# A hybrid encoder step on one core: the scan's strip products in two bursts a group, the mask by 64-row products, two small pads

## The chip, the cores and the metric

The kernel runs on one core of one Trainium2 chip. The metric is the device time of one execution in microseconds. Shown are the median of three runs and one profiled execution with its trace. PE is TensorE (its matmuls; PEld its weight loads), DVE is VectorE, ACT is ScalarE, POOL is GpSimd, SP the engine whose queue issues most DMAs.

## The reference

One layer for a prompt of 1024 rows and a sample of 64 rows that share the weights. Three head groups read one projection of the normalised input; their gated outputs go through `w_out`, and a cross-attention to 256 memory rows follows. Cut to the two parts that the change touches:

```python
def hgrn2_scan(q, k, v, g, s0):                  # 4 heads of 128
    def step(s, inp):                            # one chunk of rows
        G = jnp.cumsum(gc, axis=1)
        o = jnp.einsum('bthk,bhkv->bthv', qc * jnp.exp(G), s)
        diff = G[:, :, None] - G[:, None, :]
        decay = jnp.exp(jnp.where(causal, diff, -jnp.inf))
        att = jnp.einsum('bthk,btshk,bshk->bhts', qc, decay, kc)
        o = o + jnp.einsum('bhts,bshv->bthv', att, vc)
        s_new = jnp.exp(GL)[..., None] * s + jnp.einsum('bshk,bshv->bhkv', kc * jnp.exp(GL[:, None] - G), vc)

def sb_block(q, q_pos, k, v, k_pos):             # 4 heads of 64
    z = jnp.einsum('bqhd,bkhd->bhqk', q, k) * (B_HEAD_DIM ** -0.5)
    mask = (k_pos[None, :] < q_pos[:, None])[None, None]
    log_1m = jnp.where(mask, jax.nn.log_sigmoid(-z), 0.0)
    after = lax.cumsum(log_1m, axis=3, reverse=True) - log_1m
    w = jnp.where(mask, jnp.exp(jax.nn.log_sigmoid(z) + after), 0.0)
    return jnp.einsum('bhqk,bkhd->bqhd', w, v)
```

Beside these stand the pooling group, the memory's keys and values (`mem_kv`, sixteen blocks of `w_xk` and `w_xv`), and `cross_attn`.

## The kernel before

**Stages.** The start transposes and splits the memory rows and the inputs and makes the memory's keys and values (up to about 100 us). Then come the input projections, with the scan of each head beside them (to about 455), the stick-breaking attention beside its own projections and `w_out` (to about 690), the cross-attention (to about 836) and `w_xo`. Every wide product is done as three fp32r products of split operands: `hhi,whi`, `hlo,whi` and `hhi,wlo`, 128 rows by 384, 320 or 256 columns.

**What sets the order.** `Sched` runs generators that record instructions: `main` and spawned tasks such as `hgrn0`. It keeps a virtual time for each engine, adds a cost for each recorded instruction, and gives the next turn to the first task whose dependences are done at PE's virtual time; a task gives up its turn at each `yield`. A projection yields after every six products. `pause(0.9)` yields until PE's virtual time is 0.9 us on. A list scheduler then places the recorded instructions on each engine in its own order, by priority and readiness. Loads of weight blocks go through SP's queue into two buffers `wraw`; ScalarE makes `whi` of them, VectorE `wlo`.

**A scan group.** A head has three groups: two of four chunks of 128 rows, and the sample's one chunk of 64. `prepA` and `prepB` make the factors `E` (one tile for each level), `k`, `qf`, `Kh` on ScalarE and VectorE. `pe1a` does the strip products of the two coarse levels into `pA`. `pe1b` does those of the four fine levels and of the diagonal, 16 and 4 for a chunk, each 32 columns of weights wide, into one PSUM tile `pB` for two chunks; VectorE multiplies and reduces `pB` to blocks of `AT`, ScalarE copies `pA` into `AT`. PE then transposes `Kh`, ScalarE copies the result to `Kt`. `pe2a` multiplies `V` by `Kt` and updates the states `S`; `pe2b` multiplies `V` by `AT` and `G` by `S` and norms the result (`o_sb`); `pe3` transposes `o_sb`. Before the change, `pe1b` pauses after each chunk, and the group pauses before `pe1b`.

**The mask.** `scores` multiplies, for two heads at once, rows 0 to 63 and rows 64 to 127 of the queries and keys (three products for each of two PSUM tiles `zs`). In the unit that holds the newest keys it adds a triangle of -1e30 by a product of an identity, `identb`, with `negmask`, over all 128 rows. There are 18 such units.

**Pools.** Tiles lie one behind another in pools. `const` holds `identb` and `negmask`; `C` and the transposed inputs `hT` follow it. `start` holds `mhi` and `mlo` (the memory rows, split), `xattn` the cross-attention's tiles.

Of the kernel before, what the change touches and what calls it, by code (L numbers as in the profile page):

```python
# [8 lines left out]
F32 = mybir.dt.float32  # L9
F32R = mybir.dt.float32r  # L10
BF16 = mybir.dt.bfloat16
AF = mybir.ActivationFunctionType
ALU = mybir.AluOpType
AX = mybir.AxisListType

P = 128
# [9 lines left out]
NEG = -1e30  # L26
# [78 lines left out]
def hybrid_step(  # L105
# [102 lines left out]
    with tc.high_priority(offset=10 * URGENT):  # L208
        ones = const([P, P], F32, "ones")
        DVE.memset(ones, 1.0)  # L210
        ident = const([P, P], F32, "ident")
        make_identity(nc, ident)
        mhalf = const([P, 4], F32, "mhalf")
        POOL.memset(mhalf, -0.5)

        identb = const([P, P], BF16, "identb")
        negmask = const([P, P], BF16, "negmask")
        DVE.memset(negmask, 0.0)
        POOL.affine_select(out=negmask, in_=negmask, pattern=[[-1, P]], compare_op=ALU.is_gt,
                           fill=NEG, base=0, channel_multiplier=1)  # L220
        cur["masks"] = (identb, negmask)
        blkmask = const([P, 4], F32, "blkmask")
        DVE.memset(blkmask, 0.0)
        for i in range(4):
            DVE.memset(blkmask[32 * i:32 * i + 32, i:i + 1], 1.0)
        invw = const([P, 2], F32, "invw")
        invcnt = const([P, 2, 16], F32, "invcnt")
        for ct in range(2):
            POOL.iota(invcnt[:, ct, :], pattern=[[1, 16]], base=1, channel_multiplier=0,
                      allow_small_or_imprecise_dtypes=True)  # L230
            for g in range(2):
                w = float(2 << (2 * ct + g))
                rs = slice(64 * g, 64 * g + 64)
                DVE.memset(invw[rs, ct:ct + 1], 1.0 / w)

    def late_constants(pool):
        wpl = pool([P, 2, P], F32, "wpl")
        DVE.memset(wpl, 0.0)
        DVE.tensor_copy(identb, ident)
        for ct in range(2):  # L240
            for g in range(2):
                rs = slice(64 * g, 64 * g + 64)
                DVE.tensor_scalar(out=invcnt[rs, ct, :], in0=invcnt[rs, ct, :], scalar1=float(2 << (2 * ct + g)),
                                  scalar2=None, op0=ALU.min)
        DVE.reciprocal(invcnt, invcnt)
        for g in range(4):
            rs = slice(64 * (g % 2), 64 * (g % 2) + 64)
            POOL.dma_start(wpl[rs, g // 2, rs], w_pool[0, g])
        onorm = const([P, 4], F32, "onorm")
        POOL.dma_start(onorm, hgrn_onorm_g)  # L250
        pscale = const([P, 2], F32, "pscale")
        POOL.dma_start(pscale, pool_scale)
        cur["hgrn"] = (blkmask, onorm)
        cur["pool"] = (invw, invcnt, wpl, pscale)
# [109 lines left out]
    def hgrn(h, st, hp, hgc):  # L364
# [103 lines left out]
        def pe1b(gi):  # L468

            t0, width, csz, v0 = groups[gi]  # L470
            nch, nq = width // csz, csz // 32
            x = ctxs[gi]
            E, k, qf, pA = x["E"], x["k"], x["qf"], x["pA"]
            AT = hp([P, 4, P], F32, "AT", 1)
            for c0 in range(0, nch, 2):
                cn = min(2, nch - c0)
                pB = ps_hg()[:, :384].rearrange("p (c l t) -> p c l t", l=6, t=32)
                for c in range(cn):
                    o = (c0 + c) * csz
                    for li, b in enumerate(FINE):  # L480
                        for i in range(nq):
                            sl = slice(o + 32 * i, o + 32 * i + 32)
                            mm(pB[32 * i:32 * i + 32, c, li, :], E[b][:, sl], E[b][:, sl], True, True)
                    for i in range(nq):
                        sl = slice(o + 32 * i, o + 32 * i + 32)
                        mm(pB[32 * i:32 * i + 32, c, 4:6, :], k[:, sl], qf[:, :, sl], True, True)
                    yield from pause(0.9)
                msk = hp([P, 2, 6, 32], F32, "msk")
                tt(msk[:csz, :cn].rearrange("p c l t -> p c (l t)"),
                   pB[:csz, :cn].rearrange("p c l t -> p c (l t)"),  # L490
                   fmask[:csz].rearrange("p l t -> p (l t)").unsqueeze(1).broadcast_to([csz, cn, 192]), ALU.mult)
                dg = hp([P, 2, 32], F32, "dg", 2)
                sch.op("DVE", 0.07 + cn * 192 / 960.0)
                DVE.tensor_reduce(out=dg[:csz, :cn], in_=msk[:csz, :cn].rearrange("p c l t -> p c t l"), axis=AX.X,
                                  op=ALU.add)
                tt(AT[:csz, c0:c0 + cn, :csz].rearrange("p c (i t) -> p c i t", t=32),
                   dg[:csz, :cn].unsqueeze(2).broadcast_to([csz, cn, nq, 32]),
                   blkmask[:csz, :nq].unsqueeze(1).unsqueeze(3).broadcast_to([csz, cn, nq, 32]), ALU.mult)
            if csz == P:
                act(AT[0:64, :nch, 64:128], pA[0:64, :nch, 64:128], AF.Copy)  # L500
            for s in range(0, csz, 64):
                act(AT[s:s + 32, :nch, s + 32:s + 64], pA[s:s + 32, :nch, s + 32:s + 64], AF.Copy)
            pk = ps_tp()
            for c in range(nch):
                tr(pk[:csz, c * P:(c + 1) * P], x["Kh"][:, c * csz:(c + 1) * csz], P)
            Kt = hp([P, 512], F32, "Kt")
            act(Kt[:csz, :nch * P], pk[:csz, :nch * P], AF.Copy)
            x["AT"], x["Kt"] = AT, Kt
# [62 lines left out]
        yield None  # L571
        pe1a(0)
        beside(prepA, 1)
        yield from pause(0.9)
        yield from pe1b(0)
        yield None
        pe2a(0, None)
# [7 lines left out]
        pe1a(1)  # L585
        beside(prepA, 2)
        factors_of(1)
        yield from pause(0.9)
        yield from pe1b(1)
        yield None  # L590
        pe2a(1, ctxs[0]["S"][-1])
# [7 lines left out]
        yield None  # L599
        pe1a(2)  # L600
        sch.done[("wide", h)] = 0.0
        yield from pause(0.9)
        yield from pe1b(2)
        yield None
        pe3(1)
# [2 lines left out]
        yield None  # L608
        pe2b(2)
        SP.dma_start(s_hgrn[0, 0, h], ctxs[2]["S"][-1])  # L610
        yield None
        pe3(2)

    def sb_all(ops, pool):
# [14 lines left out]
        def scores(u):  # L629
            (qh, ql), (kh, kl), vb, cv = ops[u["pair"]]  # L630
            i, n, nq = u["i"], u["n"], _rows(u["i"])
            u["s"], u["m"] = [], []
            zs = [ps_hg(), ps_hg()]
            qs = slice(i * P, i * P + nq)
            ks = slice(u["base"] + u["s0"], u["base"] + u["s0"] + n)
            for pi, (q, k) in enumerate(((qh, kh), (qh, kl), (ql, kh))):
                for e in range(2):
                    own = slice(64 * e, 64 * e + 64)
                    mm(zs[e][:nq, :n], q[own, qs], k[own, ks], pi == 0, pi == 2 and not u["first"])
            if u["first"]:  # L640
                for z in zs:
                    mm(z[:nq, n - nq:n], cur["masks"][0][:nq, :nq], cur["masks"][1][:nq, :nq], False, True)
            for e, z in enumerate(zs):
                s = pool([P, 512], F32, "sm", 7)
                m = pool([P, 512], F32, "sm", 7)
                act(m[:nq, :n], z[:nq, :n], AF.Sigmoid, scale=-0.125)
                act(s[:nq, :n], z[:nq, :n], AF.Sigmoid, scale=0.125)
                p = None if u["first"] else u["before"]["m"][e]
                sch.op("DVE", 0.07 + n / 480.0)
                DVE.tensor_tensor_scan(m[:nq, :n][:, ::-1], m[:nq, :n][:, ::-1], m[:nq, :n][:, ::-1],  # L650
                                       1.0 if p is None else p[:nq, 0:1], ALU.mult, ALU.min)
                if p is not None:
                    tt(s[:nq, n - 1:n], s[:nq, n - 1:n], p[:nq, 0:1], ALU.mult)
                tt(s[:nq, :n - 1], s[:nq, :n - 1], m[:nq, 1:n], ALU.mult)
                u["s"].append(s)
                u["m"].append(m)
# [76 lines left out]
    def main():  # L733
# [155 lines left out]
        g1 = pool([P, D], F32, "g1")  # L889
        g1row = pool([33, D], F32, "rows")[32:33]  # L890
        gT = pool([P, KT], F32, "gT")
        with tc.high_priority(offset=10 * URGENT):
            with nc.allow_non_contiguous_dma("one column per 128 of the norm's weights"):
                ACT.dma_start(gT, norm_mem.rearrange("o (k p) -> p (o k)", p=P))
            ACT.dma_start(g1row, norm_mix_pre)
# [434 lines left out]
        for h in range(4):  # L1330
# [14 lines left out]

            sch.fresh()
            kv = load_kv(h)
            wbs = [xw.pop(2 * h), xw.pop(2 * h + 1)]
            for c, (t0, n) in enumerate(CHUNKS):
                n1 = min(n, SEQ - t0)  # L1350
# [109 lines left out]
```

## Time and profile before

| | |
|---|---|
| median of three runs | 935.03 us (934.71 to 935.86) |
| the profiled execution | 935.02 us, its span 933.3 us |
| instructions | 18372 |
| PE busy | 914.2 us, 98% of the span |
| VectorE, ScalarE, POOL busy | 556.6, 479.5, 107.2 us |
| granted TensorE clock | 0.996 |
| DMA | 73.60 MB, 79 GB/s in the mean |

The span runs from the first to the last instruction; the execution's own time holds 1.7 us more. A row of the timeline gives the start, the duration, the engine and line, the operation, the tile written and those read, the rows and columns of a product with its shape, and the count of like instructions in a row. The ends of matmuls are modelled, and they overlap. In the trace a product of fp32 operands (`hg<-E`, `hg<-qf,k`, `hg<-V,Kt`) stands as two instructions, one of fp32r operands as one.

### The profile page before, as it was taken

The page shows a single profiled execution, that of the slowest core. Times are in us where ns is not written, and L with a number is a line of the kernel's source. Part 1 is how long each engine was busy: PE and PEld are TensorE (multiplying, and loading weights), DVE is VectorE, ACT ScalarE, POOL GpSimd, SP SyncE. Part 2 cuts the span into 40 slices and gives each one's busy share as a digit, 9 for nine tenths or more (in the row PEclk, how much of TensorE's full clock was granted, in tenths as well). Part 3 has the DMA queues.
Part 4 walks back from the last instruction along what each step waited for, and adds up shares of the span by engine and source line. Part 5 has one row for each costly group of instructions (what it writes and reads, how often), then busy time and mean ns, then how long its engine had stood idle before and what let it go on. Part 6 is the DMA issues. An engine that isn't in the chain of part 4 may idle for free.

```text
span 933.3 us, 18372 instructions
## 1 busy us (share of the span) xinstructions
PE 914.2 (98%) x7504; PEld 853.6 (91%) x7504; DVE 556.6 (60%) x1125; ACT 479.5 (51%) x1005; POOL 107.2 (11%) x194
## 2 busy tenths in 40 slices
PE   8899999999999999999999999999999999999997
PEld 7899999999998999989779788999999999999997
DVE  6849483674678574552684777565564545563343
ACT  7623384658767774963673765433452333342231
POOL 5502430010010010000000000211200000001110
PEclk9999999999999999999999999999999999999999
DMA  8815511011100111012111411222433111232231
GB/s 306 259 38 181 142 46 47 25 49 29 47 27 31 47 33 46 25 47 79 47 31 36 157 61 69 90 68 80 164 119 92 30 39 46 76 106 91 91 101 58
DMA packets 33126, 73.60 MB, mean 79 GB/s; under 512 B 5601, under 2 KB 18065, under 8 KB 33042
## 3 DMA queue, kind: packets, MB, share of 16 engines
q1 hardware_dynamic: 30112, 68.07, 22.7%
q0 software_dynamic: 1888, 4.35, 1.3%
q8 instruction: 59, 0.97, 0.4%
q14 instruction: 25, 0.20, 0.1%
q10 hardware_dynamic: 1042, 0.01, 0.1%
HBM read 56.45 MB, written 15.89 MB: 78 GB/s over the span
## 4 chain that ended last, share of the span: by engine, by line
PE 82%; DVE 6%; ACT 4%; DMA 4%; issue 2%; POOL 1%; DVEq 0%; POOLq 0%; ACTq 0%
PE mm L171 64%; PE hg L171 14%; PE tp L175 5%; DVE sm L650 3%; DVE sm L187 1%; DVE wlo L187 1%; ACT L183 1%; ACT whi L183 1%; DMA xt<-in_x_prompt_dram 1%; DVE hlo L187 1%; DMA wraw<-in_w_xk_dram 1%; DMA mkd<-mraw 1%; DMA wraw<-in_w_xo_dram 1%; DMA gT<-in_norm_mem_dram 1%; DMA mvd<-mtm 1%
## 5 line engine op out<-in xcount | busy, mean ns | idle before, releaser
L171 PE MATMUL mm<-hhi,whi 128*128 128x384 f32 (+2 forms) x1272 | 425.1, 334 | 0.0
L171 PE MATMUL mm<-hlo,whi 128*128 128x384 f32 (+2 forms) x1272 | 412.5, 325 | 0.0
L171 PE MATMUL mm<-hhi,wlo 128*128 128x384 f32 (+2 forms) x1248 | 405.3, 325 | 0.0
L171 PEld LDWEIGHTS mm<-hhi,whi 128*128 128x128 f32 x1272 | 239.2, 188 | 6.3 <-issue 1.3
L171 PEld LDWEIGHTS mm<-hlo,whi 128*128 128x128 f32 x1272 | 239.5, 188 | 1.2 <-issue 0.9
L171 PEld LDWEIGHTS mm<-hhi,wlo 128*128 128x128 f32 x1248 | 234.6, 188 | 0.4 <-issue 0.3
L187 DVE TENSOR_TENSOR wlo<-wraw,whi 128x1024 fp32r<-128x1024 f32 (+1 forms) x53 | 63.5, 1200 | 56.6 <-ACT whi L183 56.3
L183 ACT ACT_TABLE_LOAD x66 | 84.7, 1283 | 19.0 <-DVE E L187 12.0
L183 ACT ACTIVATE whi<-wraw 128x1024 fp32r<-128x1024 f32 (+1 forms) x53 | 55.3, 1043 | 71.5 <-PE mm L171 54.7
L183 ACT ACTIVATE wraw<-mm 128x384 f32<-128x384 f32 (+3 forms) x51 | 22.9, 449 | 72.8 <-PE mm L171 62.9
L650 DVE TENSOR_TENSOR_SCAN sm<-sm 128x384 f32<-128x384 f32 (+4 forms) x52 | 48.3, 938 | 14.0 <-ACT sm L183 14.0
L183 ACT ACTIVATE sm<-hg 128x384 f32<-128x384 f32 (+4 forms) x104 | 42.2, 485 | 15.7 <-PE hg L171 8.7
L187 DVE TENSOR_TENSOR wraw<-mm,gain 128x384 f32<-128x384 f32 (+1 forms) x48 | 24.4, 510 | 41.6 <-ACT wraw L183 41.3
L1241 POOL TENSOR_TENSOR small<-small 128x1 f32<-128x1 f32 (+1 forms) x18 | 4.2, 234 | 375.3 <-ACT wraw L183 375.3
L183 ACT ACTIVATE E<-E 128x512 f32<-128x512 f32 (+1 forms) x68 | 32.8, 515 | 10.5 <-DVE E L187 9.9
L171 PE MATMUL mm<-mhi,wlo 128*128 128x256 f32 x128 | 35.8, 289 | 1.8 <-DVE wlo L187 1.8
L321 POOL TENSOR_TENSOR small<-small,mhalf 128x1 f32<-128x1 f32 (+2 forms) x50 | 36.0, 719 | 4.2
L171 PE MATMUL mm<-mhi,whi 128*128 128x256 f32 x128 | 36.2, 293 | 0.1
L171 PE MATMUL mm<-mlo,whi 128*128 128x256 f32 x128 | 35.1, 283 | 0.0
L443 POOL COPY qf<-q 128x512 f32<-128x512 f32 (+1 forms) x12 | 14.6, 1218 | 177.6 <-PE hg L171 140.7
L187 DVE TENSOR_TENSOR wlo<-C,whi 128x1024 fp32r<-128x1024 f32 x16 | 19.6, 1225 | 24.9 <-ACT whi L183 23.4
L191 DVE SCALAR_TENSOR_TENSOR C<-wraw,small,C 128x384 f32<-128x384 f32 (+3 forms) x54 | 27.8, 569 | 10.2 <-POOL small L321 10.2
(209 smaller groups left out, 1409.1 us busy)
## 6 DMA issues: line engine op xcount, KB each, us to landing
wraw<-in_w_in_dram SPq DMA_DIRECT2D x28, 512.0 KB, 3.6
xt<-in_x_prompt_dram SPq DMA_DIRECT2D x8, 512.0 KB, 6.5
wraw<-in_w_xv_dram SPq DMA_DIRECT2D x8, 512.0 KB, 3.9
wraw<-in_w_out_dram SPq DMA_DIRECT2D x8, 512.0 KB, 3.6
C<-in_x_prompt_dram SPq DMA_DIRECT2D x8, 512.0 KB, 3.5
x1d<-C SPq DMA_DIRECT2D x8, 512.0 KB, 2.8
wraw<-in_w_xq_dram SPq DMA_DIRECT2D x8, 512.0 KB, 3.6
wraw<-in_w_xo_dram SPq DMA_DIRECT2D x8, 512.0 KB, 3.6
```

The lines of the kernel that those rows point to most:

```text
L171: cur['PE'] = PE.matmul(out, lhsT=lhsT, rhs=rhs, start=start, stop=stop, skip_group_check=True)
L175: PE.transpose(out, in_, ident[:n, :n])
L183: cur['ACT'] = ACT.activation(out, in_, func, **kw)
L187: cur['DVE'] = DVE.tensor_tensor(out=out, in0=a, in1=b, op=op)
L191: DVE.scalar_tensor_tensor(out=out, in0=a, scalar=s, in1=b, op0=op0, op1=op1)
L321: POOL.tensor_tensor(out=r[:n, :w], in0=r[:n, :w], in1=mhalf[:n, :w], op=ALU.pow)
L443: POOL.tensor_copy(qf[:, 1, :], qq)
L650: DVE.tensor_tensor_scan(m[:nq, :n][:, ::-1], m[:nq, :n][:, ::-1], m[:nq, :n][:, ::-1], 1.0 if p is None else p[:nq, 0:1], ALU.mult, ALU.min)
L1241: POOL.tensor_tensor(out=ms[:n, 0:1], in0=ms[:n, 0:1], in1=ms[:n, pi:pi + 1], op=ALU.add)
```

## The change

`pe1b` pauses once, between the two pairs of chunks, and no longer after every chunk; the pauses ahead of it go (in the second group a plain `yield` stays). Before the sample's last transposes, `pe3(2)`, the task becomes ready 0.7 us after its latest dependence. The mask is added by products of 64 rows: `picks` holds two selections of the identity, one for each half of 64 key columns, in rows 0 to 63 and again in rows 64 to 127. The second also holds a row of ones, which gives the first 64 queries a row of the mask that is -1e30 throughout. `negmask` is 64 columns wide. Two tiles that nothing reads are set to zero: `step` (32 bytes a row) in `start`, behind `gT`, and `xstep` (64 bytes) in `xattn`, ahead of `qhi`.

```diff
-        identb = const([P, P], BF16, "identb")
-        negmask = const([P, P], BF16, "negmask")
+        picks = const([P, 2, P], BF16, "picks")
+        negmask = const([P, 64], BF16, "negmask")
         DVE.memset(negmask, 0.0)
-        POOL.affine_select(out=negmask, in_=negmask, pattern=[[-1, P]], compare_op=ALU.is_gt,
-                           fill=NEG, base=0, channel_multiplier=1)
+        for e in range(2):
+            POOL.affine_select(out=negmask[64 * e:64 * e + 64], in_=negmask[64 * e:64 * e + 64], pattern=[[-1, 64]],
+                               compare_op=ALU.is_gt, fill=NEG, base=0, channel_multiplier=1)
...
-        DVE.tensor_copy(identb, ident)
+        DVE.memset(picks, 0.0)
+        for e in range(2):
+            es = slice(64 * e, 64 * e + 64)
+            for i in range(2):
+                DVE.tensor_copy(picks[es, i, 64 * i:64 * i + 64], ident[es, es])
+            DVE.memset(picks[64 * e:64 * e + 1, 1, 0:64], 1.0)
...
                         mm(pB[32 * i:32 * i + 32, c, 4:6, :], k[:, sl], qf[:, :, sl], True, True)
+                if c0 + 2 < nch:
                     yield from pause(0.9)
...
         pe1a(0)
         beside(prepA, 1)
-        yield from pause(0.9)
         yield from pe1b(0)
...
         factors_of(1)
-        yield from pause(0.9)
+        yield None
         yield from pe1b(1)
...
         pe1a(2)
         sch.done[("wide", h)] = 0.0
-        yield from pause(0.9)
         yield from pe1b(2)
...
         SP.dma_start(s_hgrn[0, 0, h], ctxs[2]["S"][-1])
+        sch.cur.dep["EV"] = max(sch.cur.dep.values()) + 0.7
         yield None
         pe3(2)
...
             if u["first"]:
-                for z in zs:
-                    mm(z[:nq, n - nq:n], cur["masks"][0][:nq, :nq], cur["masks"][1][:nq, :nq], False, True)
+                picks, negmask = cur["masks"]
+                for hf in range(nq // 64):
+                    for e in range(2):
+                        own = slice(64 * e, 64 * e + 64)
+                        c0 = n - nq + 64 * hf
+                        mm(zs[e][:nq, c0:c0 + 64], picks[own, hf, :nq], negmask[own], False, hf == nq // 64 - 1)
...
+        POOL.memset(pool([P, 8], F32, "step"), 0.0)
...
+            if h == 0:
+                POOL.memset(xq([P, 16], F32, "xstep"), 0.0)
```

PE's order before, in the first group of head 0 (`E`, `qf` and `k` are the strip products' operands, `mm` the projection beside them), from the end of `pe1a` to the first product with `AT`:

```order
L171 MATMUL hg<-E 32x32 x2
L171 MATMUL mm<-hhi_105,whi 128x384
...
L171 MATMUL mm<-hhi_105,wlo 128x384
L171 MATMUL hg<-E 32x32 x16
L171 MATMUL hg<-qf,k 32x64 x4
L171 MATMUL mm<-hhi_105,whi 128x384
...
L175 MATMUL tp<-ident,Kh 128x128 x4
...
L171 MATMUL hg<-V,Kt 128x128 x4
...
L171 MATMUL hg<-V,AT 128x128 x2
```

Each chunk's 20 strip products stand alone here, between six projection products on either side.

PE's order in the same place now:

```order
L171 MATMUL hg<-E 32x32 x18
L171 MATMUL hg<-qf,k 32x64 x4
L171 MATMUL hg<-E 32x32 x16
L171 MATMUL hg<-qf,k 32x64 x4
L171 MATMUL mm<-hhi_108,whi 128x384
...
L171 MATMUL mm<-hhi_108,wlo 128x384
L171 MATMUL hg<-E 32x32 x16
...
L175 MATMUL tp<-ident,Kh 128x128 x4
...
L171 MATMUL hg<-V,Kt 128x128 x4
...
L171 MATMUL hg<-V,AT 128x128 x2
```

The bursts that stood apart by six projection products each now stand in two, and the transposes of `Kh` follow the second directly; from there to the product with `AT` PE had 24 projection products between the last burst and it, and has 14 now.

PE's order before, in a masked scoring unit of the attention (`wT` are the weights of an earlier unit, transposed):

```order
L171 MATMUL hg<-kl,qh 128x512 x2
L171 MATMUL hg<-kh,ql 128x512 x2
L171 LDWEIGHTS identb
L171 MATMUL hg<-negmask,identb 128x128
L171 LDWEIGHTS identb
L171 MATMUL hg<-negmask,identb 128x128
L171 MATMUL hg<-wT,vb 64x128 x4
```

Both mask products span all 128 rows, between score products over 64 rows and value products.

And now:

```order
L171 MATMUL hg<-kl,qh 128x512 x2
L171 MATMUL hg<-kh,ql 128x512 x2
L171 LDWEIGHTS picks
L171 MATMUL hg<-negmask,picks 128x64
L171 LDWEIGHTS picks
L171 MATMUL hg<-negmask,picks 128x64
L171 LDWEIGHTS picks
L171 MATMUL hg<-negmask,picks 128x64
L171 LDWEIGHTS picks
L171 MATMUL hg<-negmask,picks 128x64
L171 MATMUL hg<-wT,vb 64x128 x4
```

Two products over 128 rows have become four over 64 rows, which alternate between rows 0 to 63 and rows 64 to 127. Nothing else moved there. On SP, one load of a block of `w_in` has moved behind the loads of the post-norm's gain, `ck` and `cv`, which wait for the end of the scan's pool.

More of the change, by code (lines that the diff above doesn't have):

```diff
@@ L214, in hybrid_step @@
         POOL.memset(mhalf, -0.5)
-        identb = const([P, P], BF16, "identb")
-        negmask = const([P, P], BF16, "negmask")
+        picks = const([P, 2, P], BF16, "picks")
+        negmask = const([P, 64], BF16, "negmask")
         DVE.memset(negmask, 0.0)
-        POOL.affine_select(out=negmask, in_=negmask, pattern=[[-1, P]], compare_op=ALU.is_gt,
-                           fill=NEG, base=0, channel_multiplier=1)
-        cur["masks"] = (identb, negmask)
+        for e in range(2):
+            POOL.affine_select(out=negmask[64 * e:64 * e + 64], in_=negmask[64 * e:64 * e + 64], pattern=[[-1, 64]],
+                               compare_op=ALU.is_gt, fill=NEG, base=0, channel_multiplier=1)
+        cur["masks"] = (picks, negmask)
         blkmask = const([P, 4], F32, "blkmask")
```

## The prediction

> **What bounds the kernel now.** First the page (busy shares, slices, chain), then the busy time by stage, then the PE timeline row by row.
>
> ```profile
> PE 914.2 (98%) x7504; PEld 853.6 (91%) x7504; DVE 556.6 (60%) x1125; ACT 479.5 (51%) x1005; POOL 107.2 (11%) x194
> PEclk9999999999999999999999999999999999999999
> PE 82%; DVE 6%; ACT 4%; DMA 4%; issue 2%; POOL 1%; DVEq 0%; POOLq 0%; ACTq 0%
> 266.00:329.00 63.00, 62.64 (x747) 56.69 (x746) 46.24 (x111) 45.22 (x91) 5.40 (x9) 1.00 0.12 38
> 690.00:836.00 146.00, 145.57 (x948) 139.87 (x948) 83.19 (x205) 55.38 (x140) 0.00 (x0) 1.00 0.22 69
> ```
>
> The last two rows give a stretch, its length, the busy time of PE, PEld, DVE, ACT and POOL, the granted clock and DMA's share. TensorE is busy in 98% of the span, at full granted clock, and the chain runs through it for 82%. In these stretches (one scan head; the cross-attention) PE idles 0.4 us each. So time is won or lost by what PE itself takes, and a busy PE is not PE at its peak: a product's listed 0.34 us overlaps the next. What a product costs is the distance from its start to the next start.
>
> **The scan's bursts.** The PE timeline in one scan group (start, duration, instruction, count):
>
> ```profile
> 186.22 0.34 PE L171 MATMUL mm<-hlo,whi 128*128 128x384 f32 x1
> 186.39 0.34 PE L171 MATMUL mm<-hhi,wlo 128*128 128x384 f32 x1
> 186.66 0.46 PE L171 MATMUL hg<-E 128*32 128x32 f32 x32
> 186.94 0.34 PE L171 MATMUL hg<-qf,k 128*32 128x64 f32 x8
> 187.21 0.44 PE L171 MATMUL mm<-hhi,whi 128*128 128x384 f32 x1
> 187.49 0.34 PE L171 MATMUL mm<-hlo,whi 128*128 128x384 f32 x1
> 187.66 0.34 PE L171 MATMUL mm<-hhi,wlo 128*128 128x384 f32 x1
> 415.47 0.28 PE L171 MATMUL hg<-qf,k 128*32 128x64 f32 x3
> 415.68 0.30 PE L175 MATMUL tp<-ident,Kh 128*64 128x128 f32 x1
> ```
>
> A wide product follows a wide one after 0.17 us (186.22, 186.39; 187.49, 187.66). From 186.39 to 187.49 pass 1.10 us; the two wide products in it take 0.35, so one burst of strip products costs 0.75. Its 40 instructions themselves take 0.28 to 186.94, and at the same pace some 0.14 for the last 8: 0.42. The other 0.33 us is entering (0.27 in place of 0.17), leaving (about 0.15 after the last strip product) and a slow first wide product (0.28). It is paid per interruption, not per strip product.
>
> The order of the built programs has 47 such bursts before, 24 now (per head 12, now 6): 23 x 0.33 = 7.6 us. Eleven times more than before, the transposes of Kh follow a burst directly. Leaving a burst is still paid there (415.47 to 415.68: 0.21 for three qf products and the exit), but the slow wide product of a separate exit goes, 0.28 - 0.17 = 0.11: 11 x 0.11 = 1.2. **Bursts: -8.8 us.** Bounds: nothing if the price hangs on each strip product, and -10.5 if leaving towards transposes were free too (11 x 0.15 more). I take the middle because its terms are read directly from these rows. The same strip products still run, and ScalarE's and VectorE's work in these groups keeps its size; only the order changes (table loads fall from 66 to 54, on an engine busy 51%).
>
> **The mask.** A scoring unit with the mask, and one without:
>
> ```profile
> 554.79 0.40 PE L171 MATMUL hg<-kh,ql 64*128 64x512 f32 x2
> 555.13 0.29 PE L171 MATMUL hg<-negmask,identb 128*128 128x128 bf16 x2
> 555.34 0.55 PE L171 MATMUL hg<-wT,vb 128*64 128x128 f32 x6
> 565.93 0.40 PE L171 MATMUL hg<-kh,ql 64*128 64x512 f32 x2
> 566.26 0.88 PE L171 MATMUL hg<-wT,vb 128*64 128x128 f32 x12
> ```
>
> From the last score pair to the values 0.55 us pass with the mask, 0.33 without: it costs 0.22, half of it a change from 64 rows to 128 and on to 64 columns in place of one change. Now there are four products of 64 rows and 64 columns, in the rows' own split. A score pair of 512 columns needs 0.23 (the kl,qh and kh,ql rows of one unit lie that far apart), so a side-by-side pair of 64 columns streams in 0.03 at the least: two pairs 0.06. At the worst each costs as the 128-row ones with their exit, 0.21 for two, 0.42 for four. I take 0.10, near the lower end, for the pairs need no new split. Of 18 masked units 12 are followed by values: 12 x 0.12 = 1.4. Six are followed by a transpose or a wide product, which split like the old mask and unlike the new one: there one change replaces another, about 0. Some of this falls where PE waits for the scans of VectorE anyway: **-1.3 us**, bounds -2.3 and +3.7 (all 18 at either end).
>
> The Trainium skill, TensorEngine Tiling (Array Packing), section Instruction Overhead, speaks against it: every matmul carries some 60 cycles, so a small dimension should not be split further. Read as 60 columns at the 0.23 us per 512 above, four small products would cost 0.11 us rather than 0.06 (an estimate from that page), and the sum would be 0.6 us higher. The 32 strip products above start 0.28 us / 32 = 9 ns apart, so the trace does not show that overhead for products in different strips.
>
> **The pads.** 32 and 64 bytes move tiles. 256-column products of the same shape, first and last of runs:
>
> ```profile
> 632.95 0.28 PE L171 MATMUL mm<-hhi,whi 128*128 128x256 f32 x1
> 634.88 0.28 PE L171 MATMUL mm<-hhi,wlo 128*128 128x256 f32 x1
> 838.36 0.28 PE L171 MATMUL mm<-hhi,whi 128*128 128x256 f32 x1
> 841.10 0.28 PE L171 MATMUL mm<-hhi,wlo 128*128 128x256 f32 x1
> 706.43 0.28 PE L171 MATMUL hg<-KTh,qhi 128*128 128x256 f32 x1
> 706.91 0.28 PE L171 MATMUL hg<-KTl,qhi 128*128 128x256 f32 x1
> 83.76 0.28 PE L171 MATMUL mm<-mhi,whi 128*128 128x256 f32 x1
> 86.12 0.28 PE L171 MATMUL mm<-mhi,wlo 128*128 128x256 f32 x1
> ```
>
> 17 steps in 1.93 us are 114 ns; 23 in 2.74 are 119; 4 in 0.48 are 120; 20 in 2.36 are 118. The build places streamed and loaded operand, modulo 128 bytes, at 32 and 96 in the fast run; at 96 and 96, 32 and 32, and 64 and 96 in the other three. So 64 bytes apart is the fast case. The first pad moves mhi and mlo from 64 to 32 against weights at 96; the second, with the constants grown by 128, moves qhi and qlo to 96 against KTh at 32: both become the fast case; the other shifted tiles move by 128. Gain: 192 products of KT x 5.5 ns = 1.1 us; the P products, moved likewise, 48 of 256 columns, at 4 ns, 0.2; of the 384 with mhi and mlo, 1.5 at 4 ns, a third, 0.5, since that stage waits for weights and their splits between. **-1.8 us**, bounds 0 and -2.8. The two memsets sit on POOL, busy 11%; the second waits for PE's last read of the old tile there, and the norm behind it waits for a later product of the same row tile: nothing.
>
> The Trainium skill, TensorE: Matmul & The Clock Gate, section Step-by-step: what each phase is for, says that loading the next weights takes no read bandwidth from the running matmul. By that rule the offset could not matter and this term is 0; the trace has 114 against 120 ns.
>
> **Waits that go or come.**
>
> ```profile
> 220.25 0.27 PE L175 MATMUL tp<-ident,o_sb 64*128 64x64 f32 x1 [0.28 <-DVE o_sb L187]
> 421.81 0.27 PE L175 MATMUL tp<-ident,o_sb 64*128 64x64 f32 x1 [0.55 <-DVE o_sb L187]
> 264.75 0.49 PE L171 MATMUL hg<-V,Kt 128*128 128x128 f32 x2 [0.35 <-ACT Kt L183]
> 325.33 0.94 PE L171 MATMUL hg<-V,Kt 128*128 128x128 f32 x6 [0.25 <-ACT Kt L183]
> 234.20 0.34 PE L171 MATMUL hg<-qf,k 128*32 128x64 f32 x8
> 235.94 0.41 DVE L187 TENSOR_TENSOR E<-M,G 128x256 f32<-128x256 f32 x1
> 237.64 0.42 DVE L187 TENSOR_TENSOR AT<-dg,blkmask 128x256 f32<-128x256 f32 x1
> 238.10 0.82 ACT L183 ACTIVATE AT<-hg 64x256 f32<-64x256 f32 x3
> 239.19 0.60 PE L171 MATMUL hg<-V,AT 128*128 128x128 f32 x4
> 417.43 0.33 SPq L286 DMA_DIRECT2D wraw<-in_w_in_dram  x1
> 422.11 0.33 SPq L281 DMA_DIRECT2D gain<-in_norm_mix_post_dram  x1
> ```
>
> The later transposes of the sample take away 0.28 and 0.55; I keep **-0.6**. What comes: between a group's last strip product and its V,AT product VectorE and ScalarE make AT; in this row set that ends at 238.92, 4.6 us after the qf row, other factors (E) in between. In the new order of head 0 there lie between them 4 transposes (0.5 with the exit), 14 wide products (2.4 and two slow firsts, 0.2) and four V,Kt (0.9): 4.0. So about 0.6 is missing there. Like places: three first groups (14 to 16 wide products there; the fourth has 24) at 0.5, four of the sample's (12) at 0.2; V,Kt, with 6 to 12 wide products behind the transposes as before, keeps waits like the two above. **+2.0 us** beyond those, bounds 0 (fewer table loads make ScalarE early) and +6 (0.5 us at all twelve groups). SP's queue: one weight load, issued at 417.43, now stands behind the gain's load, which waits for the scan pool (422.11). Its block is used from 433 on: covered; uncovered it would be the 4.7 us between these rows.
>
> **Sum.** -8.8 - 1.3 - 1.8 - 0.6 + 2.0 = -10.5. The profiled execution took 935.02 us (span 933.3 and 1.7 around it), the median shown is 935.03, so no correction: **924.5 us**.
>
> **Rivals.** (a) The pads do nothing: 926.3. For: an effect of 5 ns, read off four runs of tiles. Against: each run is even to a nanosecond. (b) The change does not do what it says, half of the burst's price staying inside the longer bursts (their outputs share two banks): 4.4 less, 929. Against: the strip products of one burst already lie 9 ns apart. (c) VectorE (46 of 63 us in a head) becomes the bound of the scan, half the freed time returning as waits: 930. (d) Slower: V,Kt and V,AT come due before their evacuations in every group, because projections no longer stand between the bursts. Place: the twelve groups' V,Kt. It decides from 12.5 / 12 = 1.04 us of new waiting per group on. With 0.35 seen at worst it would need three times that; at 1.6 each, the time is 935 - 12.5 + 19 = 941.5.
>
> **Chances.** Forecast 0.57, (a) 0.2, (b) 0.08, (c) 0.08, (d) 0.07. Faster by over 0.2% (1.9 us, about what separates a measurement here from no change) hold all but (d) and a tail of (c): 0.91; within 0.2%: 0.03; slower 0.06. Range: bursts fully saved without new waits give 919; (c) and the larger wait give 931: 918.5 to 931.
>
> **What the profile after would show.** Bursts of 36 to 56 strip products, wide products 0.28 only after 24 of them, and the first Kh transpose 0.2 after the last qf; 0.43 instead of 0.55 us from kh,ql to wT; 114 ns between KT products; shorter idle before the 64-column o_sb transposes; idle with ACT Kt or AT before V,Kt and V,AT of not over 3 us together. I am wrong if the intervals inside the bursts grow, if V,AT waits a microsecond per group, or if the saved time stands as idle before the strip products.

## The result and the profile after

The changed kernel took 944.84 us (median of 4 runs, 942.36 to 949.02) against 935.44 for the kernel before: 1.0106 of its time, 95% interval 1.0068 to 1.0143. A second set of runs gave 939.76 against 934.52, 1.0049 (1.0032 to 1.0066). It is slower, by 5 to 9 us, where 924.5 had been forecast. The profiled execution was the longest of the first set: 949.02 us, span 947.3. The four executions of the first set had mean granted clocks of 0.985, 0.991, 0.992 and 0.986, the six of the second 0.992 to 0.996, and the difference of the two means, 0.0055 of some 940 us, is about the 5 us between the medians (an estimate).

The page after: busy time of the engines, granted clock in 40 slices, and the chain; then two stretches as shown of before (the same 63 us of the scan, and the cross-attention, 13.5 us later).

```profile
PE 916.2 (97%) x7536; PEld 859.8 (91%) x7536; DVE 557.8 (59%) x1131; ACT 465.2 (49%) x993; POOL 106.7 (11%) x197
PEclk9999999999999999999999689999999999999998
PE 80%; DVE 8%; ACT 6%; DMA 3%; issue 2%; POOL 1%; POOLq 0%; DVEq 0%; ACTq 0%
```

```profile
266.00:329.00 63.00, 59.45 (x717) 55.84 (x713) 39.71 (x88) 38.70 (x70) 3.75 (x6) 1.00 0.12 37
703.50:849.50 146.00, 145.27 (x951) 139.63 (x952) 83.76 (x207) 55.44 (x140) 0.00 (x0) 1.00 0.22 69
```

In the scan PE now idles 3.55 of 63 us where it idled 0.36; the cross-attention is nearly as full as it was (0.73 of 146 us idle, 0.43 before). In the chain PE has 2% less, VectorE and ScalarE 2% more each, and one slice shows a granted clock of 0.6, the next 0.8. The waits of PE (us in total, times, longest):

```profile
PE hg L171 <- ACT Kt L183: 4.9, 4, 2.1
PE hg L171 <- ACT AT L183: 4.2, 4, 1.7
PE tp L175 <- DVE o_sb L187: 1.2, 1, 1.2
```

Before, Kt was waited for 0.6 us in all and AT not at all; o_sb 0.8 in two waits. These 9.1 us at Kt and AT are 8.5 more than before, where the prediction had put 2.0 more. One of them, on PE, then what ScalarE and VectorE did in the same microseconds:

```profile
182.40 0.34 PE L171 MATMUL mm<-hhi,whi 128*128 128x384 f32 x1
184.84 1.16 PE L171 MATMUL hg<-V,Kt 128*128 128x128 f32 x8 [2.09 <-ACT Kt L183]
182.75 1.28 ACT L183 ACT_TABLE_LOAD   x1 [2.94 <-DVE E L187]
184.04 0.26 ACT L183 ACTIVATE E<-E 128x64 f32<-128x64 f32 x1
184.20 0.58 ACT L183 ACTIVATE Kt<-tp 128x512 f32<-128x512 f32 x1
178.03 1.29 DVE L191 SCALAR_TENSOR_TENSOR L<-fl,L 128x1088 f32<-128x1088 f32 x1 [2.27 <-ACT L L183]
179.36 1.29 DVE L187 TENSOR_TENSOR fl<-L,fl 128x1088 f32<-128x1088 f32 x1
182.38 0.18 DVE L187 TENSOR_TENSOR E<-M,G 128x32 f32<-128x32 f32 x1
```

The transposes of Kh end at 181.0, and the copy to Kt takes 0.58 us. But ScalarE takes its work in order, and ahead of Kt stand the first factors of the *next* group (E, 64 columns here) with the table load for their exponential. Their input comes from VectorE, which first finishes the next head's logs (1088 columns, 1.29 us twice) and this group's `msk` and `AT` blocks. So ScalarE stands idle for 2.94 us with the copy behind it that PE waits for.

The wait costs more than itself. Two stretches of 3.41 us with waits, each with the stretch that follows it, the second of these 20.48 us long (columns as in the rows above; the last three are PE clock, DMA share, GB/s):

```profile
331.15:334.57 3.42, 1.33 (x12) 1.01 (x10) 2.36 (x10) 2.98 (x8) 0.00 (x0) 1.00 0.01 2
334.57:337.98 3.41, 3.41 (x14) 3.31 (x14) 2.43 (x8) 1.86 (x5) 0.00 (x0) 0.50 0.02 5
525.71:529.13 3.42, 2.21 (x14) 1.61 (x13) 2.02 (x2) 1.95 (x5) 0.00 (x0) 1.00 0.31 78
529.13:549.61 20.48, 20.48 (x89) 13.96 (x88) 13.12 (x21) 10.29 (x24) 0.00 (x0) 0.50 0.24 75
```

After each the clock is halved, and it stays so for 3.41 us, or six times that. The first stretch had 2.09 us of idle, the second only 1.21, so that the second case is not explained by the waits alone; it is taken up below. Of the 14.0 us by which this span is longer, 1.8 were there when the scan began (the half clock of the start lasted longer; in the second set's profile the scan began 1.3 us earlier than in before), 2.4 come from the scan, 9.3 from the scoring between 508 and 600 us, where the clock is halved, 0.5 go again behind it, and the time after PE's last product adds 1.0.

### The profile page after: what moved, and what is told of

Read it like the earlier page. It is cut to its first block, busy times and chain, and to the rows that moved or that the text cites. A ratio compares the mean times of both kernels' runs of the same rounds, so it can differ in the third digit from the quotient of the medians.

```text
span 947.3 us, 18427 instructions
## 1 busy us (share of the span) xinstructions
PE 916.2 (97%) x7536; PEld 859.8 (91%) x7536; DVE 557.8 (59%) x1131; ACT 465.2 (49%) x993; POOL 106.7 (11%) x197
## 4 chain that ended last, share of the span: by engine, by line
PE 80%; DVE 8%; ACT 6%; DMA 3%; issue 2%; POOL 1%; POOLq 0%; DVEq 0%; ACTq 0%
PE mm L171 60%; PE hg L171 14%; PE tp L175 6%; DVE wlo L187 1%; ACT whi L183 1%; ACT L183 1%; DMA wraw<-in_w_out_dram 1%; DVE sm L662 1%; DVE dg L503 1%; ACT L L183 1%; DVE E L187 1%; DMA xt<-in_x_prompt_dram 1%; DVE msk L187 0%; DMA mvd<-mtm 0%; DMA wraw<-in_w_xv_dram 0%
## 5 line engine op out<-in xcount | busy, mean ns | idle before, releaser
L187 DVE TENSOR_TENSOR hlo<-tp,hhi 128x512 fp32r<-128x512 f32 (+1 forms) x36 | 22.7, 656 | 19.1 <-ACT hhi L183 19.1
```

The source lines that it names most:

```text
L187: cur['DVE'] = DVE.tensor_tensor(out=out, in0=a, in1=b, op=op)
```

## The experiments

**Each part alone.** The bursts alone (the diff's four edits of the pauses), the mask alone, the two pads alone, and everything but the bursts.

> The kernel before with the strip bursts of the change alone; mask, pads and the sample's last transposes as before. Theory 1 (the bursts bring V,Kt and V,AT in front of their evacuations; the waits of up to 2.1 us there eat the saving, and a stretch of 3.4 us with so much idle in it halves the granted clock): this kernel alone is slower than before, 936 to 948 us, with over 8 us of PE idle at Kt and AT together in the scan and at least one half-clock stretch between 150 and 560 us. Theory 2 (the mask is to blame: its products of 64 rows keep less of TensorE busy, and the half clock of 529 to 550 us lies among them): full clock in the scoring stage, and 930 to 938 us.

> The kernel before with the mask of four 64-row products alone. Theory 1: 932.5 to 934.5 us (0.13 us less from kh,ql to the next product for each of 18 units is 2.3, some of it under waits), full clock throughout, as before. Theory 2: a half-clock stretch of several microseconds between 490 and 560 us, and 940 us or more.

> The kernel before with the two pads alone. Both theories: 933.2 to 934.6 us; 256-column products of KT and of P 114 ns apart in place of 118 to 120. A rival for this part: the start is 2.3 us later in the changed kernel's profile (the half clock there ends at 13.7 us, not 11.5), and if that comes from the first pad's memset the time is 936 to 937 us.

> The changed kernel with the bursts undone: mask, pads and the later transposes of the sample stay. Theory 1: 930.5 to 933.5 us (mask -2, pads -1.3, transposes up to -0.6), full clock from 12 us to the last microseconds. Theory 2: 938 to 945 us with the half clock of the scoring stage still there.

| kernel | median us | ratio to before, 95% interval |
|---|---|---|
| bursts alone | 938.72 | 1.0042 (1.0026 to 1.0058) |
| mask alone | 935.64 | 1.0007 (0.9995 to 1.0019) |
| pads alone | 932.93 | 0.9979 (0.9963 to 0.9994) |
| all but the bursts | 935.85 | 1.0014 (0.9996 to 1.0033) |

The bursts alone are slower by 4.1 us (934.67 for the kernel before in this set), with the same waits, a new one without a releaser ("issue"), and two halved stretches, each right behind a stretch with 2.07 us of idle:

```profile
PE hg L171 <- ACT Kt L183: 4.8, 4, 2.1
PE hg L171 <- ACT AT L183: 3.3, 4, 1.6
PE hg L171 <- issue: 1.5, 2, 0.9
```

```profile
179.34:182.75 3.41, 1.34 (x10) 1.01 (x9) 2.60 (x10) 2.73 (x7) 0.00 (x0) 1.00 0.02 5
182.75:186.17 3.42, 3.42 (x16) 3.32 (x15) 2.23 (x8) 2.11 (x6) 0.00 (x0) 0.50 0.00 0
```

The other three run at full clock through the scan in their profiled executions. Theory 1 holds for the bursts; the second theory, that the mask alone halves the clock, falls. But the mask alone gave nothing that can be told from no change, where 932.5 to 934.5 us were expected, and all but the bursts took 935.85 where 930.5 to 933.5 were expected. The pads alone came out just below their range (932.93; 933.2 to 934.6), and their rival, a start made later by the first pad's memset, falls with that: the half clock of the start ended at 13.62 us there too. The mask's own gain is there, in a unit of the same kind as the one shown of before:

```profile
553.46 0.39 PE L171 MATMUL hg<-kh,ql 64*128 64x512 f32 x2
553.69 0.23 PE L171 MATMUL hg<-negmask,picks 64*128 64x64 bf16 x4
553.85 0.88 PE L171 MATMUL hg<-wT,vb 128*64 128x128 f32 x12
```

0.39 us from the scores to the values in place of 0.55. Over the 12 units followed by values the mean falls from 0.49 to 0.37 us: 1.5 us. Against it: PE's waits for VectorE at these places grow by 0.4 us, and the time from PE's last product to the end grew from 6.1 to 7.1 us (so it did in all but the bursts and in the changed kernel, and in no other; in these three a transfer of 8 KB on an instruction queue lies 4.4 to 4.5 us behind the last product, but that it is the cause is not shown). The 128 bytes that the mask's constants grew by moved other tiles too, as the pads do; that is the next point.

**Where tiles lie.** Products of KT, first and last of 17 steps, in before and in the kernel with the pads alone; then wide products of 384 columns, first and last of 53 steps, in before, with the mask alone, and in the kernel with more pads (below). Rows from three timelines of PE:

```profile
721.46 0.28 PE L171 MATMUL hg<-KTh,qhi 128*128 128x256 f32 x1
723.50 0.28 PE L171 MATMUL hg<-KTh,qlo 128*128 128x256 f32 x1
430.67 0.34 PE L171 MATMUL mm<-hhi,whi 128*128 128x384 f32 x1
439.93 0.34 PE L171 MATMUL mm<-hhi,wlo 128*128 128x384 f32 x1
```

```profile
721.75 0.28 PE L171 MATMUL hg<-KTh,qhi 128*128 128x256 f32 x1
723.67 0.28 PE L171 MATMUL hg<-KTh,qlo 128*128 128x256 f32 x1
```

```profile
430.05 0.34 PE L171 MATMUL mm<-hhi,whi 128*128 128x384 f32 x1
439.24 0.34 PE L171 MATMUL mm<-hhi,wlo 128*128 128x384 f32 x1
```

```profile
426.66 0.34 PE L171 MATMUL mm<-hhi,whi 128*128 128x384 f32 x1
435.91 0.34 PE L171 MATMUL mm<-hhi,wlo 128*128 128x384 f32 x1
```

KT goes from 120 to 113 ns a step, as forecast. But the 384-column products, for which the prediction had no term, go from 174.7 to 173.4 with the mask and back to 174.5 with more pads: in the mean 1.2 ns over some 1200 of them before 580 us, 1.4 us. And the 256-column products of the mixer's output, 114.7 ns in the mean before, take 117.8 with the mask in (192 of them, 0.6 us), unless further pads are laid (below). The prediction had the mask's 128 bytes down as harmless.

**The waits taken away.** Two cures of different kinds. One leaves the order of issue and lets the planner count V,Kt and V,AT as due later, so that other wide products are put ahead of them:

```diff
+        sch.cur.dep["EV"] = max(sch.cur.dep.values()) + 2.0   # before the yield ahead of each pe2a and pe2b
         yield None
         pe2a(0, None)
```

The other issues the next group's factors behind this group's evacuations:

```diff
-        beside(prepA, 1)
         yield from pe1b(0)
+        beside(prepA, 1)
```

(and the same for prepA(2) and pe1b(1)). The third kernel here is the kernel before with ten stops put in, to see what halves the clock.

> The changed kernel, but the planner counts V,Kt and V,AT as due 2 us later than its own estimate, so that 16 to 30 wide products stand ahead of most of them where 6 to 12 do now. Theory 1 (the bursts themselves save some 8 us, as in the intervals of the trace, and it is only the waits at Kt and AT with the half clock after them that eat it): idle at Kt and AT together under 2 us (9.1 in the changed kernel), full clock through the scan, 925 to 931 us. Theory 2 (VectorE and ScalarE can't make the factors any faster, so the waits only move): the idle stands before the strip products of the next group, the o_sb transposes or the wide products' weights instead, and the time stays at 938 us or more.

> The changed kernel, but the next group's first factors are issued behind the evacuations of this group (prepA after pe1b), so that AT and Kt no longer stand behind a table load and factors in ScalarE's and VectorE's queues. Theory 1 (the queues' order is what makes AT and Kt late): idle at Kt and AT together under 3 us, no half clock in the scan, 926 to 934 us. Theory 2 (the evacuations take as long in any order): idle at Kt and AT stays at 7 us or more, 940 us and above.

> The kernel before with ten stops put in: nine in the output projection of the cross-attention (wide products alone), one ahead of the scoring of the second pair's third row tile. Each stop is a transpose, a copy on VectorE, 2 to 9 copies of 128 columns one after another on GpSimd, and a transpose of the last one; from GpSimd's 1.2 us for 512 columns some 0.3 us each, so stops of about 1.4 to 3.5 us. Theory A (the granted clock is set for each stretch of 3.41 us by how much TensorE did in the one before): a stop that puts over 2.0 us of idle into one stretch halves the clock for the next, one of under 1.7 does not, and a longer stop cut in two by a stretch's border may pass; among wide products the half clock lasts one stretch, and after the stop in the scoring, whose products keep less of TensorE busy, several (20.5 us in the changed kernel). Theory B (any stop over about a microsecond may halve it, at random): halved and unhalved stretches do not sort by idle.

Later due times: 926.42 us, 0.9910 (0.9890 to 0.9931). Factors behind: 928.32, 0.9931 (0.9911 to 0.9950). Against the changed kernel's second set that is 13.3 and 11.4 us less, and neither has a halved stretch between the start and the end. With the factors behind, the whole of what is waited for at Kt and AT is

```profile
PE hg L171 <- ACT Kt L183: 0.3, 1, 0.3
```

At the place shown above, four rows of this kernel, of VectorE, ScalarE and PE:

```profile
175.93 1.28 DVE L187 TENSOR_TENSOR fl<-L,fl 128x1088 f32<-128x1088 f32 x1
182.42 1.28 ACT L183 ACT_TABLE_LOAD   x1 [3.37 <-DVE E L187]
183.88 0.58 ACT L183 ACTIVATE Kt<-tp 128x512 f32<-128x512 f32 x1
184.51 1.16 PE L171 MATMUL hg<-V,Kt 128*128 128x128 f32 x8
```

The table load and the factors still stand ahead of the copy to Kt. But VectorE has done the next head's logs by 177.2, well ahead of the burst, and its E comes 0.3 us after the group's last strip product began, where it came 2.5 us after in the changed kernel. So Kt is there 2.35 us after that product in place of 4.59, and the same holds at the other wait of 2.09 us (329 to 333 us in the changed kernel). The work keeps its size (ScalarE is busy 465.2 us in the changed kernel and 466.9 in this one, VectorE 557.8 and 558.1), and as many wide products lie ahead of V,Kt there (11, and 10 in the changed kernel). For the long waits at Kt, then, it is the order in the queues, VectorE's above all, that made them. For AT this is not shown. In the first groups of the first and third heads, which have 2.8 of the 4.2 us, AT comes 5.76 and 5.22 us after the last strip product with the factors behind, and 5.78 and 5.19 in the changed kernel; the wait went because 36 wide products in place of 14 stand ahead of V,AT, so there theory 2's premise, that AT takes as long in any order, holds. In the other two AT does come earlier (4.48 for 5.34, 3.19 for 4.50). With later due times 18 to 26 wide products stand ahead of V,Kt in all groups but the last (6 to 12 in the changed kernel), and cover all but 0.3 us of the longest delay, a Kt that comes 5.87 us after the last strip product. The times that theory 2 gave, 938 us or more and 940 and above, are missed by both.

The stops (one execution, 964.66 us): stretches of the last output projection with a stop in them and the one behind, then the two stops' ends on PE.

```profile
887.58:890.99 3.41, 2.36 (x16) 2.04 (x14) 1.85 (x3) 1.42 (x3) 2.12 (x5) 1.00 0.02 5
890.99:894.40 3.41, 1.94 (x12) 1.95 (x13) 1.55 (x3) 0.00 (x0) 1.35 (x4) 1.00 0.68 228
894.40:897.82 3.42, 3.42 (x21) 3.42 (x20) 0.56 (x1) 0.58 (x2) 0.00 (x0) 1.00 0.23 79
942.19:945.61 3.42, 1.40 (x9) 1.08 (x8) 1.98 (x4) 0.00 (x0) 2.72 (x7) 1.00 0.18 65
945.61:949.02 3.41, 3.41 (x13) 3.41 (x12) 0.00 (x0) 0.00 (x0) 0.00 (x0) 0.50 0.27 94
```

```profile
892.46 0.33 PE L175 MATMUL tp<-ident,e 128*128 128x128 f32 x1 [2.52 <-POOL e L283]
945.29 0.33 PE L175 MATMUL tp<-ident,e 128*128 128x128 f32 x1 [2.02 <-POOL e L283]
```

A stop of 2.52 us, cut by a border into 1.05 and 1.46, leaves the clock full. One of 2.02 us that lies within one stretch halves the next. Of the ten stops three halved the clock. The borders are those of a fixed grid: in one trace all changes of the clock lie a whole number of 3.413 us apart (334.57 and 529.13 above: 57). Over all traces, behind the start, seven stretches with 2.0 us or more of idle were each followed by a halved one; outside the scoring none with up to 1.86 was. Theory A holds outside the scoring. The Trainium skill, TensorE: Matmul & The Clock Gate, section What's actually happening, has this window (free-running, 3413 ns, half clock after an idle one): the traces agree on the grid and the length. Its section on HAM oscillation puts the limit at idle gaps of over about 3.4 us; here 2.02 us are enough, and the measurement decides. The part of the theory on the scoring falls: the stop there was followed by two halved stretches, 6.83 us, not six.

**The change again, without the mask, and with more pads.** The last two have the later due times, 128 bytes behind the constants and 64 behind the second norm's tiles; the fourth also has the factors behind the evacuations, and 1 us in place of 2.

> The changed kernel once more, unaltered, beside the two below. Theory 1 (the half-clock stretches follow from waits in the schedule): waits at Kt and AT of 8 to 10 us as in its first profile, half clock again after the stretches with 2 us of idle, 942 to 946 us. Theory 2 (the 20.5 us of half clock in the scoring, 10 us lost, was one execution's accident and not the kernel's): the scoring runs at full clock this time, and the median is 938 to 940 us.

> The changed kernel with the mask undone (the 128-row mask products as before), bursts, pads and later transposes kept. The bursts alone measured +4.1 us and all but the bursts +1.2, 5.3 together where the whole change measured +9.4: about 4 us come from the combination. Theory 1 (the mask's thin products leave too little work in the scoring's stretches, so that a wait halves the clock there): 936 to 938 us (bursts +4.1, pads -1.7), full clock after 400 us. Theory 2 (the mask has no part in it): 941 us or more, half clock in the scoring as in the changed kernel.

> The kernel with V,Kt and V,AT counted 2 us later (926.4 us), and two more pads: 128 bytes behind the constants, which puts the streamed tiles of the output projection's 256-column products back where they were before the mask's constants grew, and 64 bytes behind the second norm's tiles, which moves the streamed tiles of the cross-attention's output projection to 64 bytes below the loaded ones, modulo 256. Theory 1 (a 256-column product takes 114 ns where the loaded operand lies 64 bytes above the streamed one modulo 256, and 116 to 120 elsewhere): 118 to 114 ns for 192 products, 116 to 114 for the 192 of KT, 119.4 to 114 for the 208 of the last projection: 0.7 + 0.3 + 1.1 = 2.1 us less, 924.3. Theory 2 (only the distance modulo 128 counts, or none): 926.4 us, 118 and 119.4 ns stay.

> As the kernel before it in this list, but with the next group's factors issued behind the evacuations (928.3 us by itself) and only 1 us more for V,Kt and V,AT. Theory 1 (either cure takes the waits away, both together nothing more): 923 to 926 us. Theory 2 (the factors issued late make the next group's strip products late, so the cures add up to less): 927 us or more.

The changed kernel again: 939.76. The waits are nearly the same (4.9 us at Kt and 3.2 at AT), the 20.5 us of half clock are not there. One stretch is halved in the scan, behind 2.09 us of idle, and one in the scoring, behind 1.45:

```profile
179.67:183.08 3.41, 1.32 (x11) 1.30 (x11) 2.22 (x9) 3.33 (x11) 0.00 (x0) 1.00 0.00 0
183.08:186.49 3.41, 3.41 (x15) 3.35 (x14) 2.20 (x7) 1.82 (x4) 0.00 (x0) 0.50 0.00 0
459.56:462.97 3.41, 1.96 (x18) 1.45 (x17) 3.41 (x7) 2.53 (x7) 0.00 (x0) 1.00 0.54 160
462.97:466.39 3.42, 3.42 (x20) 2.76 (x21) 2.94 (x5) 1.67 (x4) 0.00 (x0) 0.50 0.15 42
```

The median is theory 2's, the waits and the halved stretch of the scan are theory 1's. In this set the change costs 5.2 us, which is what the bursts alone (4.1) and all but the bursts (1.2) add up to: the 4 us that seemed to come from their combination go with the lower clocks of the first set.

Without the mask: 937.56, 1.0021 (1.0006 to 1.0036), full clock throughout though 1.7 us are idle in each of two stretches. That is in theory 1's range, but its interval overlaps that of the changed kernel's second set (1.0032 to 1.0066), and eleven traces have 1.3 to 1.4 us of idle at this place of the scoring with no halving behind it, the mask in six of them. Nor do these stretches sort when transposes, too, are counted as idle: 2.12 us stood ahead of the halving at 462.97, and 2.17 to 2.45 in eight traces ahead of none. What makes 1.2 or 1.45 us enough there now and then, and what held the clock down for six stretches in one execution, stays open. It is not the bursts alone: of the executions without a trace, one of all but the bursts has a granted clock of 0.989 and takes 942.58 us.

With more pads: 930.37, 0.9942 (0.9920 to 0.9965), 4 us more than without them, where 2.1 less were expected (the two intervals just overlap). Of the three groups only the mixer's output came out at 114 ns; KT went to 117.0, the last projection from 119.4 to 116.8, and all 384-column products got slower (173.3 to 175.0 early on, 173.5 to 175.8 at the end, means of all steps). Distance modulo 256 is not the rule either, and a pad that helps one group moves others. Both cures and the pads: 935.09, 1.0006 (0.9986 to 1.0027), with 3.6 us of waits at Kt again: the cures do not add.

**The bursts with their waits covered**, and nothing else of the change.

> The kernel before with the strip bursts of the change and V,Kt and V,AT counted 2 us later; mask, pads and the sample's last transposes as before. Theory 1 (the bursts save some 8 us of TensorE's own time, and once the waits are covered nearly all of it is seen): the kernel with everything and the later due times took 926.4; taking off what the pads gave (-1.7) and what the mask with its placement gave (between -1 and +1), 926 to 929 us, 5.5 to 8.5 less than before; idle at Kt and AT under 1.5 us, one to three stalls inside bursts. Theory 2 (the saving seen there came from mask, pads and placement): 932 us or more.

926.65 us, 0.9917 (0.9904 to 0.9931): 7.8 less than before (934.41 in this set) from the bursts with later due times, without the rest of the change. What is left at Kt is 0.3 us, and a stop inside one burst:

```profile
PE hg L171 <- issue: 1.5, 1, 1.5
PE hg L171 <- ACT Kt L183: 0.3, 1, 0.3
```

```profile
295.78 0.30 PE L171 MATMUL hg<-E 128*32 128x32 f32 x13
297.63 0.34 PE L171 MATMUL hg<-E 128*32 128x32 f32 x17 [1.55 <-issue]
```

PE's own time and its waits between the 800th and the 2240th wide product (the scan), from the distances of starts in the PE timeline, less idle and less the time at half clock (us):

| kernel | own time, full clock | waits | at half clock |
|---|---|---|---|
| before | 346.1 | 4.1 | 0 |
| bursts alone | 335.4 | 13.5 | 6.8 |
| bursts, pads, late transposes (no mask) | 338.7 | 13.3 | 0 |
| bursts alone, later due times | 336.8 | 5.5 | 0 |
| changed kernel, factors behind | 336.4 | 5.3 | 0 |
| changed kernel, first profile | 335.0 | 14.0 | 3.4 |
| all but the bursts | 344.6 | 4.5 | 0 |

## Why the prediction was wrong, point by point

- **Bursts, -8.8: held.** PE's own time in the scan falls by 7.4 (no mask) to 9.3 us (later due times), and 7.8 arrive in the measured time once the waits are covered. A slow first wide product stands behind 24 bursts now, as said: directly behind 12 of them, and behind the transposes of Kh that follow the other 12. The bound of nothing, if the price hung on each strip product, is out.
- **New waits, +2.0 with bounds 0 and +6: the step that failed.** Measured, 9.4 us more idle in the scan (4.1 to 13.5), and about 3.4 for two halved stretches on top (6.8 us at half clock, half of it lost if PE has work throughout): 12.8 for the bursts alone, 11.8 by the difference of the two measured kernels with and without later due times (+4.1 and -7.8). In the changed kernel 4.3 of the 8.5 us that came at Kt and AT stand at Kt, where the prediction had nothing beyond the waits of before. It took these over because as many wide products lie there as before; but in before a pause, six wide products at the place shown, came between the last strip products and the transposes, and ScalarE and VectorE had that time. Nor did it ask what stands ahead of Kt in the two queues: a table load, the next group's factors, and on VectorE the next head's logs. The other 4.2 stand at AT, where the mechanism was right and the term too small: the working set 4.0 us of PE's work against an AT that comes 4.6 us after the last strip product, a figure of before; in the first groups of three heads it came 5.2 to 5.8 us after in the changed kernel, and the waits were 0.9 to 1.7 us, not 0.5.
- **The clock had no term at all.** The trace of before shows full clock for 918 us, with at most 1.3 us of idle in a stretch; a sum with 9 us of new waits in pieces of up to 2.1 needed one.
- **Rival (d)** named the place, with 0.07, and half the mechanism: the products do come due before their evacuations, but in seven of the twelve groups, at V,AT as much as at V,Kt, and at the two longest waits because of the queues' order. Its threshold of 1.04 us a group, 12.5 in all, is not reached by the 8.5 us at Kt and AT; the clock and the smaller losses do the rest.
- **Mask, -1.3: held at its place** (1.5 us at 12 units, and 0.39 us where 0.43 was expected), and lost around it: 0.4 in waits, 1.0 in the tail, while the shifted tiles give 1.4 and take 0.6. These pieces add up to -0.9; the measured +0.7 (-0.5 to +1.8) is not to be told from zero, and the rest is not accounted for. The rule of the Trainium skill weighed there (TensorEngine Tiling (Array Packing), section Instruction Overhead: no small dimension split further) does not show: the unit costs 0.06 us more than one without the mask (0.33), the lower end. The 0.6 us that the prediction gave for that rule count from 0.06; its sum had taken 0.10, so 0.1 us would have been at stake.
- **Pads, -1.8: held as a sum** (-2.0, interval -3.5 to -0.6): KT 119.3 to 114.2 ns, mhi and mlo 118.2 to 116.4; P stays at 118, that part is wrong. In the changed kernel, where the mask's bytes are added, KT gets only to 116.0. "The other shifted tiles move by 128" as a reason for no effect is refuted. Rival (a), no effect of pads, is out.
- **Late transposes, -0.6: nothing.** o_sb is waited for 0.9 us in two waits without the bursts, 0.8 before.
- **SP's load, covered:** nothing in the traces speaks against it; it was not tried by itself.

## What to carry to other kernels

When a change takes work out from between a product and its consumer, list what stands ahead of each evacuation in its engine's queue, in order, and what that itself waits for, before costing the wait; the evacuation's own duration says little. If the forecast then has waits of about two microseconds on a TensorE that never stopped before, add the clock. And keep the slack where it is cheap: the same change with later due times for two products turned +5 us into -8, while a small pad that gains at one group of tiles can lose at another (-2.0 us for two alone, 4 us more with two further ones).

## What the runs showed of the hardware

- The clock is decided stretch by stretch, on a grid of 3.413 us: 2.02 us of idle in one halved the next, 2.52 us across a border did not. In the scoring 1.21 and 1.45 us were each followed by half clock once.
- TensorE seems to run out of instructions inside long bursts. The stop at 296.08 to 297.63 above begins 0.2 us before the end of a transfer of 16 KB on an instruction queue (295.39 to 296.32), and ends 1.3 us behind it. Sixteen such stops, of 0.1 to 1.6 us, stand inside the bursts in seven of the eight kernels with two bursts a group, one to three in each trace, and none in the five with the short bursts; every one of them ends 1.26 to 1.53 us after the end of such a transfer. The queue carries 59 of these transfers, all through the execution, one for about every 256 of PE's 15008 products and weight loads.
- Steps between equal products differ by where their operands lie: 113 to 120 ns at 256 columns, 173.3 to 175.8 at 384. No rule tried here (modulo 128, modulo 256) sorts them.
